# New operation costs and a shared port in the planner that orders a hybrid decoder block's instructions

## The chip, the cores and the metric

The kernel runs on one core of a Trainium2 chip. The metric is the device time of one execution in microseconds (us); lower is better. Times of the kernel before are the median of three runs. The profile shows one further execution, taken by the hardware profiler; its spans and waits are in microseconds from the first instruction.

## The reference, cut to what matters

One layer over 1024 tokens of width 1024, all in float32. The input is normalised and multiplied by one wide matrix. Its columns feed a state-space (SSD) branch of 32 heads in 8 chunks of 128 tokens, a sliding-window attention branch of 12 heads, and two gates. A SwiGLU feed-forward part follows.

```python
h = rmsnorm(x, norm_mix)
z, xBC, dt_raw, qkv, gate_logits = split(h @ w_in)
y_ssm = mamba2_branch(z, xBC, dt_raw, ...) @ w_ssm_out
y_att = dilated_attention_branch(rope(q), rope(k), v) @ w_att_out
gates = sigmoid(gate_logits + b_gate)
x = x + (gates[0] * y_ssm + gates[1] * y_att) @ w_mix_out
h = rmsnorm(x, norm_ffn)
x = x + (silu(h @ w_ffn_gate) * (h @ w_ffn_up)) @ w_ffn_down
return rmsnorm(x, norm_final)
```

## The kernel before, in words

**Arithmetic.** A float32 operand is split into a rounded high part and a low remainder, and a product is made of three TensorE (PE) matmuls over these (`mm3`). The split is a ScalarE (ACT) copy for the high part and a VectorE (DVE) subtraction for the low part. Three groups of products (`Seven` for half of the input columns and for the feed-forward columns, and the last product) use a Strassen-like scheme with seven products in place of eight. They need sums of operands, made by GpSimd (POOL) and DVE.

**Stages.** In the head, eight token tiles `xts[0..7]` of 128 x 1024 are loaded. For each pair of tiles, `stat_task` squares both on ACT with a running sum, multiplies a tile by the norm weights on POOL, and computes the inverse root on DVE in 14 steps on 128 x 2 numbers (`rsqrt_steps`; tiles rv, rt, rs). `tile_task` then scales each tile, transposes it on PE and splits it into `hhi` and `hlo`. `stat_task` of pairs 2 and 3 waits for the events h0 and h2, that is, for tiles 0 and 2 to be emitted. `first_quarter` runs the first two column tiles of the wide product pair by pair, each after its pair's tiles. When half of the tokens is there, `t_first` makes four sums on POOL (`whole`, 128 x 1024 each), and `t_rest` makes eight smaller ones for each quarter of the rest. Then come the columns in the seven-product form (about 130 to 545 us), direct column tiles with the SSD chunks and the attention heads as background (to about 1210), the merge and the mixing product (to about 1600), and the feed-forward part and its last product.

**The order.** The program is written by a planner, `Pace`. Every operation that the code emits passes through `Engine` to `Pace.note`. It asks `cost` for a duration and keeps for each engine the time at which it would be free, for each tile the time at which it would be written (`wr`) and read (`rd`), and for PE a clock `t`. Background work is a set of Python generators (`spawn`). When one yields a list of tiles, `due_at` looks up when these would be written, and the generator goes on when the clock `t` has come to that time: at `due` after every few matmuls of the foreground (`tick`), or at `idle` when the foreground waits for an event (`until`). Of those that are due, the lower `prio` number goes first. So the costs decide only in which order instructions stand in the five engines' queues. On the chip each queue runs in order and waits for its data; the planner's own times appear nowhere in the program. Which work there is, the tiling, the buffers and the order of the foreground's matmuls don't hang on the costs, except that the planner takes buffers as they are freed.

`pump` also uses the clock: it splits the next weights `SLACK` = 4.5 us after they would have landed.

Of the kernel before, what the change touches and what calls it, by code (L numbers as in the profile page):

```python
# [12 lines left out]
F32R = mybir.dt.float32r  # L13
# [4 lines left out]
PSUM = bass.MemoryType.PSUM  # L18
# [64 lines left out]
class Buf:  # L83


    def __init__(self, owner, slot, shape, dt):
        n = math.prod(shape[1:])
        v = slot.tile(dt)[:shape[0], :n]
        if len(shape) == 3:
            v = v.rearrange("p (a b) -> p a b", a=shape[1])  # L90
        elif len(shape) == 4:
            v = v.rearrange("p (a b c) -> p a b c", a=shape[1], b=shape[2])
        self.owner, self.slot, self.v = owner, slot, v
# [43 lines left out]
def _key(a):  # L137
    name = a.tensor.name if hasattr(a, "tensor") else getattr(a, "name", None)
    if name is None:
        return None  # L140
    for big, part in PARTS.items():
        if name.startswith(big) and hasattr(a, "offset"):
            return f"{big}.{part(a.offset)}"
    return name.split("__")[0]


def _free(a):
    return math.prod(a.shape[1:])


def _space(a):
    return a.space if hasattr(a, "space") else a.ap().space
# [29 lines left out]
class Pace:  # L182


    def __init__(self):
        self.t = 0.0
        self.seq = 0
        self.tasks = []
        self.parked = {}
        self.events = set()  # L190
        self.eng = dict.fromkeys(("dve", "act", "pool", "dma"), 0.0)
        self.eng["dma"] = 0.4
        self.wr, self.rd = {}, {}
        self.stall = 0.0

    def cost(self, kind, op, aps, args, kw):
        out = aps[0]
        n = _free(out)
        if kind == "pe":
            if op == "transpose":  # L200
                return 0.11
            return (max(n / 2400, 0.107) if aps[1].dtype == F32R else max(n / 600, 0.107)) + 0.0025
        if kind == "act":
            ptr = sum(1 for k in ("scale", "bias", "accum_out") if hasattr(kw.get(k), "shape"))
            return n / 1200 + 0.095 + 0.08 * ptr
        if kind == "dve":
            if op == "reciprocal":
                return n / 120 + 0.07
            if op == "tensor_reduce":
                n = _free(aps[1])  # L210
            fast = op in ("tensor_copy", "tensor_scalar") and all(_space(a) != PSUM for a in aps[:2])
            return n / (1920 if fast else 960) + 0.07
        if kind == "pool":
            return n * 0.0022 + 0.05
        return n * out.shape[0] * 4 / 360e3

    def note(self, kind, op, aps, args, kw):
        c = self.cost(kind, op, aps, args, kw)
        outs = [_key(aps[0])] + ([_key(kw["accum_out"])] if "accum_out" in kw else [])
        ins = [_key(a) for a in aps[1:]]  # L220
        s = 0.0
        for k in ins + outs:
            t, by = self.wr.get(k, (0.0, kind))
            if by != kind or (kind == "dma" and k in ins):
                s = max(s, t)
            elif kind != "pe":
                s = max(s, t - 0.025)
        for k in outs:
            t, by = self.rd.get(k, (0.0, kind))
            if by != kind:  # L230
                s = max(s, t)
        if kind == "pe":
            self.stall += max(0.0, s - self.t)
            e = self.t = max(self.t, s) + c
            lag = 0.1
        else:
            e = self.eng[kind] = max(self.eng[kind], s) + c
            lag = 2.0 if kind == "dma" else 0.15
        for k in outs:
            self.wr[k] = (e + lag, kind)  # L240
        for k in ins:
            if e >= self.rd.get(k, (0.0, ""))[0]:
                self.rd[k] = (e, kind)

    def due_at(self, bufs):
        return max(self.wr.get(_key(getattr(b, "v", b)), (0.0, ""))[0] for b in bufs)
# [1802 lines left out]
```

## Time and profile before

| what | us |
|---|---|
| median of three runs (lowest and highest) | 2247.75 (2247.21 to 2248.05) |
| the profiled execution | 2249.83 |
| its span, first to last instruction | 2248.0 |
| PE busy in it | 2162.8 |
| DVE, ACT, POOL busy | 1535.9, 877.8, 688.1 |
| mean granted TensorE clock, as a share of full speed | 0.987 |

The profile page names one source line, 165, for every operation, because a helper records them all; tiles are told apart by their names, with the buffer's number left out. A wait in brackets after an instruction is the idle time of its engine before it, with what ended it. A PE that is busy is not always at full speed: the table by stretch has a column with the granted clock.

### The profile page before, as it was taken

To read this page: it belongs to the slowest core of one execution; us is meant where nothing else is said; L and a number is where in the kernel's file an instruction comes from. 1 tells how busy PE (TensorE), PEld (TensorE's weight loads), DVE (VectorE), ACT (ScalarE), POOL (GpSimd) and SP (SyncE) were. 2 spreads that over 40 slices of the span, in tenths; PEclk is the share of its full clock that TensorE was granted. 3 is DMA by queue.
4 is the path that set the end of the run, shared out by engine and by line. 5 is a ranking of instruction groups with operands and counts; after the bars stand their busy time and mean duration, and the time that the engine had idled before them with its cause. 6 is when DMAs were issued, how large, how long until landed. Compare 5 with 4: busy or idle time off the path is not lost.

```text
span 2248.0 us, 27884 instructions
## 1 busy us (share of the span) xinstructions
PE 2162.8 (96%) x10476; PEld 1780.2 (79%) x10476; DVE 1535.9 (68%) x2094; ACT 877.8 (39%) x1565; POOL 688.1 (31%) x420
## 2 busy tenths in 40 slices
PE   4999999999999999999999999999989999999997
PEld 4877888887777778888888887888868877788885
DVE  7879898866777667654343437544796776767788
ACT  3344444434565556433332224322333222224444
POOL 5223343321554445421004003002373344420102
PEclk7999999999999999999999999999999999999998
DMA  3433334336566556431127457454233332349332
GB/s 124 125 89 117 108 116 119 104 112 206 159 191 172 160 169 187 113 94 39 38 72 233 145 178 248 127 173 135 63 108 94 104 107 80 122 155 348 106 95 98
DMA packets 302587, 299.83 MB, mean 133 GB/s; under 512 B 20028, under 2 KB 246260, under 8 KB 302196
## 3 DMA queue, kind: packets, MB, share of 16 engines
q1 hardware_dynamic: 302452, 298.05, 42.7%
q8 instruction: 82, 1.34, 0.3%
q14 instruction: 53, 0.43, 0.1%
HBM read 225.00 MB, written 73.01 MB: 133 GB/s over the span
## 4 chain that ended last, share of the span: by engine, by line
PE 72%; DVE 13%; DMA 5%; issue 4%; ACT 3%; POOL 3%; SPq 0%; DVEq 0%; POOLq 0%; ACTq 0%
DVE rt L165 1%; PE wide__40_16210 L165 1%; PE wide__39_16209 L165 1%; PE wide__39_15720 L165 1%; PE wide__38_15719 L165 1%; PE wide__32_11149 L165 1%; PE wide__33_11380 L165 1%; PE wide__31_11045 L165 1%; PE wide__4_4172 L165 1%; PE wide__29_10493 L165 1%; PE wide__32_11279 L165 1%; PE wide__41_16660 L165 1%; PE wide__35_11736 L165 1%; PE wide__34_11554 L165 1%; PE wide__28_10224 L165 1%
## 5 line engine op out<-in xcount | busy, mean ns | idle before, releaser
L165 POOL TENSOR_TENSOR xr<-xr,nfin 128x512 f32<-128x512 f32 x16 | 22.9, 1443 | 192.2 <-ACT jk L165 192.2
L165 POOL TENSOR_TENSOR slab__24_12098<-h2hi,h2lo 128x1024 f32<-128x1024 f32 x1 | 3.4, 3387 | 135.6 <-PE wide__35_11736 L165 135.6
L165 POOL TENSOR_TENSOR slab__14_10598<-slab__14_10598,last__2_10581 128x1024 f32<-128x1024 f32 x1 | 2.4, 2397 | 122.4 <-DMA slab__14_10598<-yt_d 122.4
L165 POOL TENSOR_TENSOR slab__15_4124<-slab__15_4124,slab__15_4121 128x1024 f32<-128x1024 f32 x1 | 2.3, 2349 | 63.9 <-DVE wide__3_4015 L165 63.9
L165 POOL TENSOR_TENSOR more__3_12094<-h2hi,h2lo 128x512 f32<-128x512 f32 x2 | 2.6, 1294 | 62.3 <-DVE h2lo L165 62.3
L165 POOL TENSOR_TENSOR slab__3_1140<-slab__3_1086 128x512 f32<-128x512 f32 x1 | 1.3, 1297 | 47.5 <-DVE slab__4_1089 L165 47.5
L165 ACT ACTIVATE jk<-xr 128x512 f32<-128x512 f32 x16 | 10.1, 631 | 13.1 <-DVE xr L165 12.8
L165 POOL TENSOR_TENSOR slab__7_7601<-slab__7_7601,slab__33_9400 128x1024 f32<-128x1024 f32 x1 | 2.4, 2393 | 41.0 <-DMA slab__33_9400<-fd 41.0
L165 DVE TENSOR_TENSOR rs<-rs,rt 128x2 f32<-128x2 f32 (+2 forms) x30 | 12.3, 410 | 1.0
L165 PE MATMUL wide__4_4172<-hhi,slab__15_3980 128*128 128x512 f32 x16 | 8.4, 526 | 4.6 <-DVE slab__3_4170 L165 4.6
L165 PE MATMUL bank__3_458<-ident,slab__1_154 128*128 128x128 f32 x4 | 1.1, 428 | 11.5 <-DVE slab__1_154 L165 11.5
L165 POOL TENSOR_TENSOR more__4_12528<-slab__19_12483 128x512 f32<-128x512 f32 x1 | 7.4, 7417 | 14.0 <-DVE slab__25_12501 L165 14.0
L165 ACT ACTIVATE xr<-xr,or 128x512 f32<-128x512 f32 x8 | 5.8, 721 | 14.8 <-DVE or L165 14.0
L165 POOL TENSOR_TENSOR slab__18_8210<-slab__18_8210,slab__15_4121 128x1024 f32<-128x1024 f32 x1 | 2.4, 2397 | 26.6 <-ACT slab__18_8210 L165 26.6
L165 POOL TENSOR_TENSOR slab__11_8494<-slab__11_8494,slab__15_4121 128x1024 f32<-128x1024 f32 x1 | 2.4, 2399 | 26.6 <-ACT slab__11_8494 L165 26.6
L165 POOL TENSOR_TENSOR slab__18_9053<-slab__18_9053,slab__15_4121 128x1024 f32<-128x1024 f32 x1 | 2.4, 2411 | 25.6 <-ACT slab__18_9053 L165 25.6
L165 POOL TENSOR_TENSOR slab__22_8765<-slab__22_8765,slab__15_4121 128x1024 f32<-128x1024 f32 x1 | 2.4, 2406 | 25.5 <-ACT slab__22_8765 L165 25.5
L165 PE MATMUL wide__1_183<-hhi,slab__1_250 128*128 128x256 f32 x32 | 9.8, 307 | 0.3 <-ACT hhi L165 0.3
L165 PE MATMUL wide__1_183<-hlo,slab__1_250 128*128 128x256 f32 x32 | 9.4, 294 | 0.7 <-DVE hlo L165 0.7
L165 PEld LDWEIGHTS bank__3_458<-ident,slab__1_154 128*128 128x128 f32 x4 | 0.7, 218 | 11.7 <-issue 11.7
L165 PE MATMUL wide__1_184<-hhi,slab__1_301 128*128 128x256 f32 x32 | 9.3, 290 | 0.5 <-DVE slab__1_301 L165 0.5
L165 PE MATMUL wide__1_184<-hhi,slab__1_300 128*128 128x256 f32 x32 | 9.5, 297 | 0.0
(7605 smaller groups left out, 8349.3 us busy)
## 6 DMA issues: line engine op xcount, KB each, us to landing
xr<-x_d SPq DMA_DIRECT2D x8, 512.0 KB, 5.8
out<-xr SPq DMA_DIRECT2D x16, 256.0 KB, 2.2
b_d<-hhi SPq DMA_DIRECT2D x1, 1024.0 KB
b_d<-hlo SPq DMA_DIRECT2D x1, 1024.0 KB
slab__1_150<-in_x SPq DMA_DIRECT2D x1, 512.0 KB, 4.2
slab__1_151<-in_x SPq DMA_DIRECT2D x1, 512.0 KB, 5.1
slab__1_158<-in_norm_mix SPq DMA_DIRECT2D x1, 512.0 KB, 5.9
slab__1_165<-in_w_in SPq DMA_DIRECT2D x1, 512.0 KB
```

The costliest lines, as they stand in the source:

```text
L165: r = call(*args, **kw)
```

## The change

Only `Pace` is changed; no operation, tile, wait or event is added or taken away in the code that uses it. `cost` gets other constants: a matmul of split operands on 512 columns goes from 0.216 to 0.226 us, every ACT, DVE and POOL operation gets a fixed part that is larger by about 0.08 to 0.14 us, a float32 matmul with 64 weight columns or fewer becomes cheaper, and DMA goes from 360 to 345 GB/s. A new method, `take_port`, keeps the last 40 intervals of DVE operations whose operands all lie in SBUF and of POOL operations. A new POOL operation that would overlap one of DVE's is moved behind it; a new DVE operation that would overlap one of POOL's is moved by 0.55 of the overlap that is left.

```diff
+        self.port = {k: deque(maxlen=40) for k in ("dve", "pool")}
...
+            if aps[1].dtype == F32R:
+                return max(n / 2400 + 0.0125, 0.107)
+            return max(n / 600, 0.107) * (1.0 if aps[1].shape[-1] > 64 else 0.68) + 0.0025
...
-            return n / 1200 + 0.095 + 0.08 * ptr
+            return n / 1200 + 0.18 + 0.08 * ptr + 0.1 * ("accum_out" in kw)
...
-            fast = op in ("tensor_copy", "tensor_scalar") and all(_space(a) != PSUM for a in aps[:2])
-            return n / (1920 if fast else 960) + 0.07
+            if op in ("tensor_copy", "tensor_scalar") and all(_space(a) != PSUM for a in aps[:2]):
+                return n / 1920 + 0.21
+            return n / 960 + 0.15 + 0.06 * min(ptr, 1)
         if kind == "pool":
-            return n * 0.0022 + 0.05
-        return n * out.shape[0] * 4 / 360e3
+            return n * 0.0022 + 0.15
+        return n * out.shape[0] * 4 / 345e3
...
-            e = self.eng[kind] = max(self.eng[kind], s) + c
+            s = max(self.eng[kind], s)
+            if kind == "pool" or kind == "dve" and all(_space(a) != PSUM for a in aps):
+                s = self.take_port(s, c, kind)
+            e = self.eng[kind] = s + c
...
+    def take_port(self, s, c, kind):
+        other = self.port["dve" if kind == "pool" else "pool"]
+        for a, e in other:
+            if a < s + c and s < e:
+                s += (e - s) * (0.55 if kind == "dve" else 1.0)
+        self.port[kind].append((s, s + c))
+        return s
```

## Rows read from the trace of the kernel before

**Rows 1.** Page: PE's busy time, and its share in 40 equal slices, tenths.
```profile
PE 2162.8 (96%) x10476; PEld 1780.2 (79%) x10476; DVE 1535.9 (68%) x2094; ACT 877.8 (39%) x1565; POOL 688.1 (31%) x420
...
PE   4999999999999999999999999999989999999997
```

**Rows 2.** Table by stretch: length, busy us (instructions) of each engine, PE clock, DMA, GB/s.
```profile
0.00:72.00 72.00, 42.15 (x279) 40.18 (x280) 51.13 (x90) 23.72 (x38) 37.67 (x22) 0.81 0.32 103
...
120.00:200.00 80.00, 70.56 (x292) 56.16 (x291) 67.46 (x74) 32.22 (x49) 27.68 (x16) 0.96 0.32 94
...
580.00:930.00 350.00, 339.39 (x2125) 273.76 (x2124) 249.47 (x408) 196.54 (x446) 171.42 (x124) 1.00 0.57 170
...
1380.00:1420.00 40.00, 36.06 (x157) 28.90 (x156) 27.39 (x28) 16.05 (x30) 7.04 (x3) 1.00 0.56 182
...
1600.00:1660.00 60.00, 53.21 (x274) 43.99 (x273) 57.95 (x59) 24.29 (x39) 35.97 (x18) 1.00 0.28 84
1660.00:2000.00 340.00, 336.73 (x1476) 276.12 (x1475) 246.38 (x320) 99.04 (x176) 151.35 (x104) 1.00 0.32 104
...
2210.00:2248.00 38.00, 21.43 (x77) 15.44 (x75) 29.53 (x104) 14.02 (x29) 9.31 (x8) 0.79 0.29 110
sum 2248.00, PE 2162.76 PEld 1780.21 DVE 1535.91 ACT 877.78 POOL 688.09; mean PE 166.37 PEld 136.94 DVE 118.15 ACT 67.52 POOL 52.93
```

**Rows 3.** Chain that ended last: start us, us, what (12 matmuls).
```profile
195.16 2.72 PE bank__13_1512 L165 x12
```

**Rows 4.** Timeline near 130 us: start us, us, instruction [idle before, releaser].
```profile
131.52 0.69 DVE L165 TENSOR_TENSOR slab__3_1071<-slab__2_694,slab__3_1071 128x512 fp32r<-128x512 f32 x1
...
132.58 0.62 ACT L165 CAST slab__4_1089<-slab__2_793 128x512 fp32r<-128x512 f32 x1
...
135.16 1.30 POOL L165 TENSOR_TENSOR slab__3_1140<-slab__3_1086 128x512 f32<-128x512 f32 x1 [47.52 <-DVE slab__4_1089 L165]
```

**Rows 5.** Timeline of the head, first and second pair of tiles.
```profile
15.11 1.15 ACT L165 ACTIVATE slab__1_151<-slab__1_151,rs 128x1024 f32<-128x1024 f32 x1 [4.11 <-DVE rs L165]
...
16.17 1.04 ACT L165 ACTIVATE slab__1_160<-slab__1_152 128x1024 f32<-128x1024 f32 x1
...
17.38 2.36 POOL L165 TENSOR_TENSOR slab__1_152<-slab__1_152,slab__1_158 128x1024 f32<-128x1024 f32 x1 [3.96 <-ACT slab__1_160 L165]
...
19.64 0.45 PE L165 MATMUL wide__1_183<-hhi,slab__1_250 128*128 128x256 f32 x1
...
20.89 2.39 POOL L165 TENSOR_TENSOR slab__1_153<-slab__1_153,slab__1_158 128x1024 f32<-128x1024 f32 x1 [1.15 <-DMA slab__1_143<-in_consts]
...
22.26 2.10 DVE L165 TENSOR_TENSOR slab__1_301<-slab__1_169,slab__1_300 128x1024 fp32r<-128x1024 f32 x1 [0.25 <-ACT slab__1_300 L165]
...
24.28 2.35 DVE L165 TENSOR_SCALAR rv<-sq 128x2 f32<-128x2 f32 x1
```

**Rows 6.** Timeline of the head, third and fourth pair of tiles.
```profile
37.06 2.37 POOL L165 TENSOR_TENSOR slab__1_156<-slab__1_156,slab__1_158 128x1024 f32<-128x1024 f32 x1 [8.15 <-ACT slab__1_160 L165]
...
39.49 2.31 DVE L165 TENSOR_TENSOR rs<-rs,rt 128x2 f32<-128x2 f32 x1
...
48.64 2.33 POOL L165 TENSOR_TENSOR slab__1_675<-hhi,hlo 128x1024 f32<-128x1024 f32 x1
...
48.74 2.25 DVE L165 TENSOR_TENSOR rs<-rs,rt 128x2 f32<-128x2 f32 x1
...
53.12 1.09 PE L165 MATMUL bank__3_458<-ident,slab__1_154 128*128 128x128 f32 x4 [11.54 <-DVE slab__1_154 L165]
...
56.48 1.28 POOL L165 TENSOR_TENSOR slab__1_678<-hhi,hlo 128x512 f32<-128x512 f32 x1 [5.51 <-DVE hlo L165]
...
63.92 0.63 PE L165 MATMUL bank__4_547<-ident,slab__1_156 128*128 128x128 f32 x4 [1.08 <-DVE slab__1_156 L165]
```

**Rows 7.** Waits of PE, 580 to 930: total us, times, longest.
```profile
PE bank__86_6731 L165 <- DVE slab__26_6624 L165: 1.8, 1, 1.8
...
PE bank__83_6556 L165 <- DVE half__13_6421 L165: 0.3, 1, 0.3
```

More of the change, by code (lines that the diff above doesn't have):

```diff
@@ L198, in cost @@
         n = _free(out)
+        ptr = sum(1 for v in list(args) + list(kw.values()) if hasattr(v, "shape") and _free(v) == 1 and n > 1)
         if kind == "pe":
@@ L201, in cost @@
                 return 0.11
-            return (max(n / 2400, 0.107) if aps[1].dtype == F32R else max(n / 600, 0.107)) + 0.0025
+            if aps[1].dtype == F32R:
+                return max(n / 2400 + 0.0125, 0.107)
+            return max(n / 600, 0.107) * (1.0 if aps[1].shape[-1] > 64 else 0.68) + 0.0025
         if kind == "act":
-            ptr = sum(1 for k in ("scale", "bias", "accum_out") if hasattr(kw.get(k), "shape"))
-            return n / 1200 + 0.095 + 0.08 * ptr
+            return n / 1200 + 0.18 + 0.08 * ptr + 0.1 * ("accum_out" in kw)
         if kind == "dve":
             if op == "reciprocal":
-                return n / 120 + 0.07
+                return n / 120 + 0.15
             if op == "tensor_reduce":
                 n = _free(aps[1])
-            fast = op in ("tensor_copy", "tensor_scalar") and all(_space(a) != PSUM for a in aps[:2])
-            return n / (1920 if fast else 960) + 0.07
+            if op in ("tensor_copy", "tensor_scalar") and all(_space(a) != PSUM for a in aps[:2]):
+                return n / 1920 + 0.21
+            return n / 960 + 0.15 + 0.06 * min(ptr, 1)
         if kind == "pool":
-            return n * 0.0022 + 0.05
-        return n * out.shape[0] * 4 / 360e3
+            return n * 0.0022 + 0.15
+        return n * out.shape[0] * 4 / 345e3
     def note(self, kind, op, aps, args, kw):
```

## The prediction

> **What bounds the kernel now.** Read the page's busy time and slices first [rows 1]: PE is busy for 2162.8 of 2248.0 us, and only the first and the last slice stand well below nine tenths. A change that adds and removes no work can win only PE's idle 85.2 us (2248.0 - 2162.8) and the time in which PE has the lower clock. So the second view is the table by stretch, with length minus PE busy [rows 2]: 29.9 us idle in the head (0 to 72, at a mean clock of 0.81), 9.4 in the start of the seven-product stage (120 to 200), 10.6 under the SSD chunks (580 to 930), 3.9 at the change to the mixing product (1380 to 1420), 6.8 in the start of the feed-forward part (1600 to 1660), 3.3 in its steady part (1660 to 2000), 16.6 in the tail (2210 to 2248). Together 80.5; the other 4.7 is in the stretches not shown. The third view is what ended each wait. The last is the durations of single operations, against the costs in the diff.
>
> **The new costs against the trace.** Twelve matmuls on 512 columns take 2.72 us, 0.2267 each [rows 3]; the old cost is 512/2400 + 0.0025 = 0.2158, the new 0.2258. On 512 elements the trace has 0.69 us for DVE, 0.62 for ACT, 1.30 for POOL [rows 4]; old 0.60, 0.52, 1.18, new 0.68, 0.61, 1.28. So the new planner sees what single operations take within 2%, where the old was 5 to 16% short. That is no gain by itself: the planner's times don't reach the chip, only the order does. An instruction that PE has in its queue before its data is ready stalls everything behind it; one that comes later costs nothing while other matmuls stand in between. So stalls by too early emission can go, and stalls of a foreground that has nothing else to do can't, unless DVE, ACT or POOL get another order.
>
> **Part 1, the head.** PE has no other work here, so what counts is the order on the other three engines.
> With the old costs a step of the inverse root is 0.07 us plus 0.15 of delay, less 0.025 within DVE; 14 steps end at 9.65 on the planner's clock, just before tile 2's data is due (0.4 + 0.18 + 5 loads of 1.46 + 2.0 = 9.86). So ACT scales tile 1 first and squares tile 2 after it. The trace shows it: scaling at 15.11, square at 16.17, POOL's product of tile 2 at 17.38 and of tile 3 at 20.89, the low part of the second weights at 22.26, and only then the second pair's chain, at 24.28 [rows 5].
> With the new costs a step is about 0.15 + 0.15, so 14 steps from 7.0 need at least 4.2 us and end after 11.2, and with the port they are pushed behind POOL's two operations to well after 13. Tile 2 is due at 0.4 + 0.19 + 5 x 1.52 + 2.0 = 10.2, tile 3 at 11.7, the second weights at 13.2. So squares 2 and 3, POOL's products 2 and 3 and the split of the second weights now stand ahead of the end of the first chain.
> On the chip that has a price and a gain. The price: a tiny DVE step that falls in a POOL operation takes 2.25 to 2.35 us [rows 5, 6], so two products (2.36 and 2.39) and the split (2.10) can put the first chain back by up to 6.9 us, and the first matmul from 19.64 to about 26. The gain: the second pair's chain, started at 24.28 now, starts near 16 (tile 3 due near 12, a square of 1.04, one or two POOL operations of 2.36), about 8 us earlier, and runs interleaved with the first.
> The end of the head is set by the last pair. Now the third chain runs against six POOL operations in a row, from 37.06 to 51 (two products, four sums of `t_first`): five steps from 39.49 to 48.74 take 2.3 us each, and PE waits 11.5 us for tile 4 [rows 6]. In the new order pairs 2 and 3 still wait for h0 and h2, so POOL's eight operations (four products, four sums, 8 x 2.35 = 18.8 us) still meet these chains; with tile 0 emitted near 27 they end near 46.5, and the fourth chain after them near 51, against about 63 now (its tile is transposed at 63.92). 63 - 51 = 12 is the best of it. The four sums at 56.48, 1.28 us each, can block the last steps as they do now: minus 5.1. What is left is 6.9; I take 5, because both figures rest on POOL having no pause. Bounds: the first matmul 6.9 later and nothing given back, +7; and 12 earlier, -12.
>
> The Trainium skill (SBUF — State Buffer, "SBUF: two separate sides") says that the port pair that DVE and GpSimd share is an exclusive lock, held for a whole instruction, and that the loser blocks fully. The five steps of 2.3 us agree. The change moves a DVE step by only 0.55 of what is left of POOL's operation, so by that rule it still sees several steps fit into one; the rival "ramps" below is what that would mean.
>
> **Part 2, under the SSD chunks.** The wait table of this stretch has 13 waits of PE, from 1.8 down to 0.3 us, almost all for a DVE, ACT or POOL result of a chunk or of rotary [rows 7]. Units of independent matmuls stand around them, and the PE as a whole is at 339 of 350. A chunk's chain between two PE steps has three to eight operations that the old costs make 0.08 to 0.1 us too short each, 0.3 to 0.8 in sum, before any blocking: the size of the waits. Later emission removes these. It also lengthens each chunk in the planner, but the y of the SSD is not used before the merge, hundreds of us later. I take -4 of 10.6; bounds -10 (all) and +3 (waits move to other places, about a third of today's).
>
> **Part 3, the other stretches.** In 120 to 200 and 1600 to 1660 DVE is busy for 67.5 of 80 and 58.0 of 60 us [rows 2]: it is the bound, the seven products come in a fixed order, and the work is the same. I take 0, bounds -3 and +5 for the first, -3 and +4 for the second. The steady feed-forward part idles 3.3 us in 340: -1, since its operations are as short in the old costs as the others, bounds -3 and +3. The mixing change (3.9) and the rest (4.7) I take at 0, bounds together -6 and +5. In the tail all waits are for a chain that is serial on DVE after the last matmul: 0, bounds -1 and +2. No DMA, wait or buffer is added; SP's order follows the same events, and its queue is far from full in every row of the table.
>
> **Sum.** -5 - 4 - 1 = -10 on the profiled execution's 2249.83 gives 2239.8. That execution lies 2.1 us above the median of the runs (2247.75), so for the median 2237.8, say 2238. All bounds at once are -38 and +29; they are independent stretches, so I take about half.
>
> **The rivals.**
> - *Ramps*: the order moves, but the head still ends with one DVE step for each POOL operation and the ramps stay DVE's. For it: six POOL operations back to back with the third chain [rows 6]. Against: the 13 waits under the SSD have no such limit. Part 2 alone with other small losses, -3: about 2245.
> - *Slower head*: POOL's products 2 and 3 and the second split go into the first chain, the first matmul comes at 26 in place of 19.64, and the third and fourth chains meet POOL as before, so the 6.9 us are not given back. For it: POOL idles now from 13.4 to 17.38, when the last steps of the first chain run freely. Against: the second chain's 8 us. It decides when the last pair's transposes come later than 63.92. Price +7, part 2 half gone at -2, and +1 elsewhere: 2254.
> - *All waits of early emission go*: the head gives its full 12, the SSD stretch 8, the others 3: -23, 2225. For it: the new costs are within 2%. Against: DVE at 58 of 60.
> - That the change doesn't reach the program at all is excluded: already the squares of tiles 2 and 3 change places by the arithmetic above.
>
> **How the numbers follow.** This kernel's measurement can tell 0.2%, 4.5 us, from no change: faster is below 2243.3, slower above 2252.2. Forecast 0.48 (its own range 2229 to 2247), ramps 0.16, slower head 0.26, all waits 0.10. Faster: 0.43 of the forecast, 0.10, 0.04 of the ramps, 0.01 of the slower head = 0.58. Same: 0.05 + 0.11 + 0.03 = 0.19. Slower: 0.22 + 0.01 = 0.23. A range of 2219 to 2257 leaves out 1 in 10 on either side.
>
> **What would show it.** Right: ACT's squares of tiles 2 and 3 ahead of the scaling of tile 1; the first matmul later than 19.64, the last pair's transposes before 60; under 7 us idle from the SSD's first chunk to its last; DVE still near full in both ramps. Wrong: transposes of the last pair after 64, or new PE waits of over 1 us between the chunks.

## The result, and the profile after

The changed kernel takes 2229.63 us (median of four runs, 2226.1 to 2232.08) against 2247.9 (four runs of the kernel before on the same chip): 0.9918 of it, 95% interval 0.9901 to 0.9935, or 18.3 us less. The forecast was 10 less; the sign, the likeliest case and the range held, but most of the gain is not where the forecast put it. The profiled execution is the lowest of the four, at 2226.1, so its sum reads -23.7 against the profiled execution before. The terms of single stretches below come from one profiled execution of each kernel, and the four timed runs lie 6 us apart, so terms are good to a few us at best.

The page after, as [rows 1]: the same number of counted instructions on every engine; PE is busy 8.4 us less, and the span is 23.7 us shorter.

```profile
PE 2154.4 (97%) x10476; PEld 1781.7 (80%) x10476; DVE 1545.7 (69%) x2094; ACT 879.5 (40%) x1565; POOL 690.9 (31%) x420
...
PE   5999999999999999999999999999999999999996
```

The table by stretch after, over the stretches of [rows 2] (length, busy us and instructions of PE, PEld, DVE, ACT, POOL, PE clock, DMA share, GB/s):

```profile
0.00:72.00 72.00, 41.61 (x277) 39.24 (x278) 51.84 (x90) 23.75 (x38) 36.82 (x22) 0.83 0.30 98
120.00:200.00 80.00, 73.23 (x304) 58.41 (x303) 67.42 (x76) 33.57 (x52) 31.57 (x16) 0.96 0.35 103
...
580.00:930.00 350.00, 350.00 (x2120) 287.76 (x2117) 245.09 (x376) 191.59 (x422) 164.69 (x110) 1.00 0.53 161
...
1600.00:1660.00 60.00, 53.51 (x222) 43.22 (x221) 58.52 (x63) 23.93 (x37) 26.97 (x16) 0.94 0.25 76
1660.00:2000.00 340.00, 340.00 (x1502) 281.71 (x1501) 246.76 (x319) 103.44 (x177) 147.99 (x102) 1.00 0.34 111
```

The head idles as long as before (30.4 against 29.9). Under the SSD PE does not idle at all (10.6 before), nor in the steady feed-forward part (3.3). The trap of this table: a fixed window of time holds other work in a kernel that is faster. So the stretches are cut at fixed work from here on. The 81 accumulators called `wide` come in the same order in both kernels; the first matmul of the 8th (the first direct column tile) and of the 45th (the last SSD and attention work is then done) bound the same matmuls. The table by stretch between these two, kernel before and kernel after:

```profile
553.40:1184.11 630.71, 620.10 (x3541) 507.83 (x3542) 380.61 (x573) 304.20 (x661) 228.42 (x151) 1.00 0.44 129
```
```profile
552.09:1168.20 616.11, 616.03 (x3541) 508.40 (x3542) 386.30 (x573) 302.77 (x661) 234.88 (x150) 1.00 0.44 131
```

Both have 3541 matmuls. Idle time goes from 10.61 to 0.08 us, busy time falls by 4.07: 14.6 together. The granted clock is the same. DVE and POOL are even busier than before, but PE no longer waits for them.

Where the 4.07 us lie can be read from the trace. Three matmuls of the kernel before, the last one ahead of a wait:

```profile
826.95 0.39 PE L165 MATMUL wide__10_6672<-hlo,slab__19_6322 128*128 128x512 f32 x1
827.18 0.39 PE L165 MATMUL wide__10_6672<-hhi,slab__19_6323 128*128 128x512 f32 x1
829.41 1.09 PE L165 MATMUL bank__86_6731<-slab__26_6624,half__13_6642 128*64 128x128 f32 x16 [1.84 <-DVE slab__26_6624 L165]
```

Matmuls follow each other every 0.23 us although each is shown with 0.39. Ahead of a wait the 0.39 count in full: from 827.18 to the next start it is 2.23 us, of which only 1.84 are shown as idle. Added up, the matmuls directly ahead of and behind the stretch's 23 waits take 6.5 us more, from start to start, than the median of their shape. In the changed kernel one wait is left and 0.6 us of this kind; all other matmuls take 1.8 more there. So the fall in busy time lies at the waits that have gone.

How it does so is seen in the middle of the stretch. The timeline at the first matmul of the 25th `wide` accumulator, before and after:

```profile
917.32 0.39 PE L165 MATMUL wide__13_7592<-hhi,slab__22_7279 128*128 128x512 f32 x1
```
```profile
870.10 0.40 PE L165 MATMUL wide__13_7094<-hhi,slab__21_6828 128*128 128x512 f32 x1
```

The last number of a name counts the tiles handed out so far. The same column tile now comes 47 us earlier and 498 tiles earlier: the chunks have been put back behind the foreground. Over the kernels of the next section that change the costs, this tile number and PE's idle time between the two bounds fall together: 7592 and 10.6 us before, 7588 and 9.1 in e2, 7409 and 7.3 in e3, 7341 and 1.3 in e4, 7169 and 1.7 in e8, 7094 and 0.1 in the changed kernel. Two don't fit by the number alone: e1 (7152) has 8.2, of which 6.7 are one wait of another kind, and e10 (7089) still has 3.0. At the 45th accumulator both kernels stand at tile 9454 again, the changed one 15.9 us ahead.

The next table gives each kernel's difference to the kernel before, between the first matmuls of the 5th, 8th, 45th, 75th and 76th `wide` accumulator (118.1, 553.4, 1184.1, 1611.5 and 2047.6 us before) and the end of the span, all from profiled executions; the last two columns are the timed medians' difference and the ratio's interval. Labels are those of the next section.

| kernel | head | seven products | SSD | mixing | feed-forward (start and steady part) | rest | timed | 95% interval |
|---|---|---|---|---|---|---|---|---|
| after | -0.2 | -1.1 | -14.6 | -0.6 | -4.1 | -3.0 | -18.3 | 0.9901 to 0.9935 |
| e1_costs | +0.6 | -2.7 | -4.2 | +2.0 | -5.2 | -1.5 | -8.4 | 0.995 to 0.9974 |
| e2_port | +1.1 | -5.8 | -4.1 | +4.1 | -4.7 | -1.8 | -8.9 | 0.9947 to 0.9976 |
| e3_pe | +0.8 | +6.1 | -4.2 | +3.1 | +0.7 | +1.4 | +11.0 | 1.0036 to 1.0069 |
| e4_fixed | -1.4 | -0.3 | -12.6 | +2.8 | -7.0 | -3.5 | -19.8 | 0.9901 to 0.9944 |
| e5_ssd_only | -0.4 | -1.0 | -15.2 | +1.8 | -0.6 | -0.1 | -14.3 | 0.9911 to 0.995 |
| e6_late_sums | -7.3 | +1.6 | -14.5 | -0.9 | -4.1 | -2.8 | -26.4 | 0.9861 to 0.9897 |
| e7_no_pool_head | -11.5 | -2.3 | -16.0 | -1.3 | -3.0 | -3.1 | -30.8 | 0.9843 to 0.9874 |
| e8_fixed_port | -0.2 | -2.3 | -14.1 | -2.3 | -5.8 | -2.0 | -24.0 | 0.9876 to 0.9905 |
| e9_fixed_port_head | -14.2 | -1.6 | -14.0 | -0.9 | -5.5 | -2.0 | -32.8 | 0.9833 to 0.9863 |
| e10_full_lock | +2.2 | +9.7 | -12.5 | +0.5 | -1.8 | -1.5 | -5.1 | 0.9964 to 0.9983 |
| e11_old_head | -0.4 | -1.2 | -15.3 | +2.1 | -2.5 | -3.0 | -21.6 | 0.9888 to 0.9917 |

The head after, against [rows 5, 6], in the timeline. First two pairs:

```profile
11.39 1.06 ACT L165 ACTIVATE slab__1_160<-slab__1_152 128x1024 f32<-128x1024 f32 x1 [0.29 <-DMA slab__1_152<-in_x]
...
15.76 1.21 DVE L165 TENSOR_TENSOR slab__1_257<-slab__1_169,slab__1_256 128x1024 fp32r<-128x1024 f32 x1
15.78 3.39 POOL L165 TENSOR_TENSOR slab__1_153<-slab__1_153,slab__1_158 128x1024 f32<-128x1024 f32 x1
...
20.86 1.15 ACT L165 ACTIVATE slab__1_151<-slab__1_151,rs 128x1024 f32<-128x1024 f32 x1 [5.40 <-DVE rt L165]
...
25.15 0.36 PE L165 MATMUL wide__1_183<-hhi,slab__1_242 128*128 128x256 f32 x1
```

The square of tile 2 stands at 11.39, ahead of the scaling of tile 1 (20.86), POOL's product of tile 3 and the second split lie inside the first chain, and the first matmul of the product comes at 25.15 instead of 19.64. Third and fourth pair:

```profile
36.12 2.37 POOL L165 TENSOR_TENSOR slab__1_156<-slab__1_156,slab__1_158 128x1024 f32<-128x1024 f32 x1 [4.22 <-ACT slab__1_160 L165]
...
40.80 2.39 POOL L165 TENSOR_TENSOR slab__1_670<-hhi,hlo 128x1024 f32<-128x1024 f32 x1
40.90 2.32 DVE L165 TENSOR_SCALAR rt<-rt 128x2 f32<-128x2 f32 x1
...
43.16 2.33 POOL L165 TENSOR_TENSOR slab__1_671<-hhi,hlo 128x1024 f32<-128x1024 f32 x1
43.25 2.25 DVE L165 TENSOR_TENSOR rs<-rs,rt 128x2 f32<-128x2 f32 x1
...
52.30 1.09 PE L165 MATMUL bank__3_479<-ident,slab__1_154 128*128 128x128 f32 x4 [9.50 <-DVE slab__1_154 L165]
...
63.15 1.09 PE L165 MATMUL bank__4_547<-ident,slab__1_156 128*128 128x128 f32 x4 [2.92 <-DVE slab__1_156 L165]
```

POOL's six operations still run back to back from 36.12, one 128 x 2 step of DVE for each, and the last pair is transposed at 63.15, against 63.92.

### The profile page after: what moved, and what is told of

It reads as the page before. It is cut to its first block, busy times and chain, and to the rows that moved or that the text cites. A ratio compares the mean times of both kernels' runs of the same rounds, so it can differ in the third digit from the quotient of the medians.

```text
span 2224.3 us, 27832 instructions
## 1 busy us (share of the span) xinstructions
PE 2154.4 (97%) x10476; PEld 1781.7 (80%) x10476; DVE 1545.7 (69%) x2094; ACT 879.5 (40%) x1565; POOL 690.9 (31%) x420
## 5 line engine op out<-in xcount | busy, mean ns | idle before, releaser
L165 POOL TENSOR_TENSOR slab__11_10598<-slab__11_10598,last__2_10581 128x1024 f32<-128x1024 f32 x1 | 2.5, 2501 | 122.1 <-DMA slab__11_10598<-yt_d 122.1
L165 POOL TENSOR_TENSOR slab__15_4124<-slab__15_4124,slab__14_4121 128x1024 f32<-128x1024 f32 x1 | 2.3, 2339 | 63.2 <-DVE wide__3_4015 L165 63.2
L165 POOL TENSOR_TENSOR slab__21_7103<-slab__21_7103,slab__32_9422 128x1024 f32<-128x1024 f32 x1 | 2.4, 2388 | 43.1 <-DMA slab__32_9422<-fd 43.1
L165 POOL TENSOR_TENSOR slab__3_1145<-slab__3_1086 128x512 f32<-128x512 f32 x1 | 1.6, 1554 | 43.3 <-PE bank__6_1094 L165 43.3
L165 PEld LDWEIGHTS bank__1_281<-ident,slab__1_151 128*128 128x128 f32 x4 | 0.7, 217 | 12.9 <-ACT slab__1_151 L165 12.9
L165 POOL TENSOR_TENSOR slab__22_9025<-slab__22_9025,slab__14_4121 128x1024 f32<-128x1024 f32 x1 | 2.4, 2404 | 25.8 <-ACT slab__22_9025 L165 25.8
L165 DVE TENSOR_TENSOR rt<-rt,rv 128x2 f32<-128x2 f32 (+2 forms) x30 | 9.7, 324 | 0.7
L165 PE MATMUL wide__1_183<-hhi,slab__1_242 128*128 128x256 f32 x32 | 9.5, 295 | 0.7 <-ACT hhi L165 0.7
L165 ACT ACTIVATE xr<-xr,or 128x512 f32<-128x512 f32 x8 | 5.8, 719 | 10.6 <-DVE or L165 10.5
L165 DVE TENSOR_SCALAR rv<-sq 128x2 f32<-128x2 f32 x4 | 2.4, 608 | 10.6 <-ACT slab__1_161 L165 10.6
L165 POOL TENSOR_TENSOR slab__10_8743<-slab__10_8743,slab__14_4121 128x1024 f32<-128x1024 f32 x1 | 2.4, 2406 | 22.7 <-ACT slab__10_8743 L165 22.7
```

The lines of the kernel that those rows point to most:

```text
L165: r = call(*args, **kw)
```

## The experiments

Diffs are against the changed kernel unless another is named. Every kernel was timed against runs of the kernel before on its own chip, and the chips differ; so two kernels are compared by their differences to the kernel before.

**Which costs carry the gain.** The five kernels of this part split the change.

`e1_costs`: all new costs, no port.

```diff
-            if kind == "pool" or kind == "dve" and all(_space(a) != PSUM for a in aps):
-                s = self.take_port(s, c, kind)
```

> All new constants, take_port taken out. Theory (the SSD stretch gains because honest fixed parts of ACT, DVE and POOL put PE's instructions behind their data): most of the gain stays, -12 to -18 us against the kernel before, and PE idle between 580 and 930 is under 3 us. Rival (the shared port is what matters): less than half stays, -8 to 0.

Measured 0.9962, 8.4 us less: between the two ranges. The SSD stretch gives only 4.2, because of one wait; the waits of PE, 580 to 960 (us in total, times, longest), and the timeline at the wait:

```profile
PE wide__15_7817 L165 <- DVE slab__6_7815 L165: 6.7, 1, 6.7
PE wide__8_5338 L165 <- DVE slab__4_5293 L165: 1.3, 1, 1.3
```
```profile
936.32 3.15 POOL L165 TENSOR_TENSOR slab__20_7773<-slab__20_7773,slab__15_4121 128x1024 f32<-128x1024 f32 x1 [2.64 <-ACT slab__20_7773 L165]
...
947.46 1.23 DVE L165 TENSOR_TENSOR wide__14_7589<-wide__14_7589,slab__16_4119 128x1024 f32<-128x1024 f32 x1 [0.33 <-ACT slab__20_7811 L165]
948.60 1.22 DVE L165 TENSOR_TENSOR slab__6_7815<-wide__14_7449,slab__20_7773 128x1024 f32<-128x1024 f32 x1
...
949.97 0.77 PE L165 MATMUL wide__15_7817<-hhi,slab__23_7542 128*128 128x512 f32 x1 [6.73 <-DVE slab__6_7815 L165]
```

There are two `wide` accumulators. A column tile's first matmul waits until DVE has read one of them (`wide__14_7449`) out in a rotary step. That step's other operand was there at 939.47 (936.32 + 3.15), but in DVE's queue it stands behind a step on the next accumulator, which itself had to wait for ACT. Of the chunks' waits, one of 1.3 and one of 0.2 are left (1.4 us idle from 580 to 930, as the theory has it). So the costs alone remove nearly all waits of the chunks. Why the rotary step stands so late is not shown: e4 below has no port either, and no such wait.

`e2_port`: `take_port` alone; every constant of `cost` as before.

```diff
-            return n / 960 + 0.15 + 0.06 * min(ptr, 1)
+            return n / (1920 if fast else 960) + 0.07
...
-            return n * 0.0022 + 0.15
+            return n * 0.0022 + 0.05
```

> take_port alone, old constants. Theory: 0 to -6 us, PE idle between 580 and 930 stays above 6. Rival (the port is what matters): -10 to -18, PE idle there under 4.

Measured 0.9962, 8.9 us less, again between the two ranges. Under the SSD nearly all waits stay, as the theory says, with PE busy for 340.89 of 350 in the table by stretch:

```profile
580.00:930.00 350.00, 340.89 (x2122) 276.82 (x2121) 255.70 (x412) 197.48 (x444) 173.21 (x121) 1.00 0.55 168
1660.00:2000.00 340.00, 340.00 (x1502) 281.56 (x1501) 249.42 (x321) 103.64 (x176) 151.36 (x104) 1.00 0.34 113
```

The port helps in the stretches where POOL and DVE both make sums (seven products -5.8, feed-forward -4.7). Under the SSD it takes only 1.5 of the 10.6 us of waits away, though the stretch is 4.1 shorter, and the mixing loses 4.1.

`e3_pe`: the two new matmul costs alone.

```diff
-            return n * 0.0022 + 0.15
-        return n * out.shape[0] * 4 / 345e3
+            return n * 0.0022 + 0.05
+        return n * out.shape[0] * 4 / 360e3
...
-                s = self.take_port(s, c, kind)
```

> The two PE costs alone (0.226 in place of 0.216 for a matmul on 512 columns, 0.68 of a float32 matmul on 64 weight columns). Theory: a dearer matmul makes the planner think that more time passes for each, so background instructions come earlier, not later: 0 to +6 us, PE idle between 580 and 930 at 10 or more. Rival (planner and chip must agree on PE's pace first): -5 to -12.

Measured 1.0052: slower by 11. The sign is the theory's, the reason is not. By the theory the chunks come earlier. The trace shows them later: at the first matmul of the 25th column tile 183 fewer tiles have been handed out than before the change.

```profile
903.82 0.48 PE L165 MATMUL wide__13_7409<-hhi,slab__20_7150 128*128 128x512 f32 x1
```

The SSD stretch has not more waits but fewer (4.7 us idle from 580 to 930, the stretch -4.2). The loss lies in the seven products (+6.1) and the mixing (+3.1). The cost of the 512-column matmul is nearer to the trace than before, and yet the order is worse; no run parts the two costs.

`e4_fixed`: the fixed parts of DVE, ACT and POOL alone; matmul and DMA costs as before, no port.

```diff
-            if aps[1].dtype == F32R:
-                return max(n / 2400 + 0.0125, 0.107)
+            return (max(n / 2400, 0.107) if aps[1].dtype == F32R else max(n / 600, 0.107)) + 0.0025
...
-                s = self.take_port(s, c, kind)
```

> The new costs of ACT, DVE and POOL alone; PE, DMA old, no port. Theory: -12 to -20 us, the SSD stretch as good as with the whole change or better. Rival (PE's pace or the port needed too): -6 to 0.

Measured 0.9922, 19.8 us less, as much as the whole change. The table by stretch has the SSD with 1.3 us of waits and the steady part with none; the 25th column tile comes 31 us and 251 tiles earlier than before the change:

```profile
580.00:930.00 350.00, 348.73 (x2151) 283.84 (x2151) 253.20 (x398) 196.02 (x439) 170.75 (x121) 1.00 0.56 172
1660.00:2000.00 340.00, 340.00 (x1501) 281.62 (x1500) 250.57 (x322) 103.63 (x176) 147.13 (x101) 1.00 0.35 112
```
```profile
886.71 0.80 PE L165 MATMUL wide__13_7341<-hhi,slab__22_7005 128*128 128x512 f32 x1
```

`e8_fixed_port`: these fixed parts and the port, matmul and DMA costs as before.

```diff
-                return max(n / 2400 + 0.0125, 0.107)
+            return (max(n / 2400, 0.107) if aps[1].dtype == F32R else max(n / 600, 0.107)) + 0.0025
...
-        return n * out.shape[0] * 4 / 345e3
+        return n * out.shape[0] * 4 / 360e3
```

> The new costs of ACT, DVE and POOL, with the port; PE and DMA at the old costs. Theory (the fixed parts carry the gain, the port adds little on top): -16 to -23, within 4 of the fixed parts alone. Rival (the port's -9 adds to the fixed parts' -20): -26 to -30.

Measured 0.989, 24.0 us less, between the two ranges: 5.7 us better than the whole change by the medians (2.9 by the profiled spans), which fits that the matmul and DMA costs take something back; the intervals (0.9876 to 0.9905 and 0.9901 to 0.9935) overlap, so its size is not settled.

**Where the gain is.** `e5_ssd_only`: the new costs and the port only from the start of the SSD's preparation (the first line) to the merge (the second).

```diff
+    pace.new = True
...
+    pace.new = False
```

> The new costs and the port only while the SSD and attention work is emitted (from the return of the saved half of the input to the merge); the old ones before and after. Theory (the SSD stretch gives most, and its gain stands by itself): -11 to -16 us, head and start of the seven products as before the change. Rival (the gain is made by the order that comes in from the earlier stages): -5 to 0.

Measured 0.9931, -14.3, with -15.2 in the SSD stretch and all others near their old values. The gain of this stretch stands by itself; it is not the head's order that brings it.

`e11_old_head`: the reverse for the head, old costs and no port until the seven products begin (the second line).

```diff
+        self.new = False
...
+    pace.new = True
```

> The old costs and no port until the two column tiles of the head are through and the seven-product stage begins, the changed ones after that. Theory that the head gained nothing (first matmul 5.7 later, third pair's transposes at the same time, end of the head 0.3 later): within 3 us of the changed kernel, with the first wait at 15.9 as before and the last pair's transposes at 63.9. The prediction's head term, in which the order of the head is worth 5: 4 to 6 us slower than the changed kernel.

Measured 0.9902, with 16.16 for the first transposes and 63.76 for the last pair's. Without the new head the change is not slower, by the medians 3.3 faster, with overlapping intervals. The head's new order is worth nothing.

**Why the head gave nothing.** `e6_late_sums`: POOL's four sums of the first half are emitted after those of the second half.

```diff
+            if self.tag == "in":
+                return
+            self.t_sums()
...
+            if self.tag == "in":
+                self.t_sums()
```

> The whole change, and the four POOL sums of the first half of the tokens emitted after those of the second half. Theory (the head gained nothing because these four sums, in POOL's queue behind the products, hold the third pair's chain at one DVE step per sum): the third chain ends near 43 in place of 51, the last pair is transposed near 55 in place of 63, and the total is 6 to 10 below the change, -24 to -28 against the kernel before. Rival (the chain is late by DVE's own queue): the third chain stays after 49, total within 3 of the change.

Measured 0.9879, 26.4 us less and 8.1 better than the changed kernel by the medians. In the profiled execution the head is 7.1 shorter and the seven products 2.7 longer. The same chain in the timeline:

```profile
38.99 2.40 POOL L165 TENSOR_TENSOR slab__1_157<-slab__1_157,slab__1_158 128x1024 f32<-128x1024 f32 x1
```
```profile
39.08 2.32 DVE L165 TENSOR_TENSOR rt<-rt,rv 128x2 f32<-128x2 f32 x1
...
41.44 0.17 DVE L165 TENSOR_SCALAR rt<-rt 128x2 f32<-128x2 f32 x1
...
43.22 0.16 DVE L165 TENSOR_TENSOR rs<-rs,rt 128x2 f32<-128x2 f32 x1
```
```profile
44.38 0.63 PE L165 MATMUL bank__3_479<-ident,slab__1_154 128*128 128x128 f32 x4 [1.06 <-DVE slab__1_154 L165]
```

The step that meets POOL's last product takes 2.32, and from 41.4, with POOL idle, the rest of the chain is through in 2 us at 0.16 a step. PE's 9.50 us of waiting for tile 4 become 1.06, and the last pair is transposed at 54.32.

`e7_no_pool_head`: e6, and the norm weights of tiles 2 to 7 multiplied on DVE, in the operation that scales the tile. The diff is against e6.

```diff
-            if q or i:
+            if 2 * q + i == 1:
...
-        if i == 0:
+        if i != 1:
+            yield [nm]
             nc.vector.scalar_tensor_tensor(xt.v, xt.v, rs, nm.v, ALU.mult, ALU.mult)
...
-            nc.vector.tensor_scalar(xt.v, xt.v, rs, None, ALU.mult)
```

> As the run with the late sums, and the multiplication of tiles 2 to 7 by the norm weights goes from POOL into DVE's scaling (scalar_tensor_tensor, as tile 0 has it): 1.28 in place of 0.75 us for a tile on DVE, six POOL operations of 2.4 us less. Theory (POOL's lock sets the whole head): the chains run at 0.2 us a step, the last pair is transposed before 50, the head ends near 55 in place of 72: 15 to 20 below the change, -33 to -38 against the kernel before. Rival (DMA or DVE's queue comes next): no more than 3 better than the late sums alone.

Measured 0.9858, 30.8 us less: 4.4 better than e6, but less than expected. The last pair is transposed at 48.30, as the theory has it. The timeline of POOL and the waits of PE in the head say why:

```profile
41.23 1.29 POOL L165 TENSOR_TENSOR slab__1_668<-hhi,hlo 128x512 f32<-128x512 f32 x1 [27.75 <-DVE hlo L165]
```
```profile
PE bank__1_277 L165 <- ACT slab__1_151 L165: 10.0, 1, 10.0
PE bank__4_541 L165 <- DVE slab__1_156 L165: 3.4, 1, 3.4
PE bank__6_715 L165 <- DVE slab__1_660 L165: 3.1, 1, 3.1
```

The last pair's chain still meets POOL's sums of 1.29 from 41.23 (3.4 us of waiting), and the sums that were put back now hold the weight split of a product that comes next (3.1).

`e9_fixed_port_head`: the costs of e8 with the head of e7.

```diff
-                return max(n / 2400 + 0.0125, 0.107)
+            return (max(n / 2400, 0.107) if aps[1].dtype == F32R else max(n / 600, 0.107)) + 0.0025
...
+            if 2 * q + i == 1:
```

> The fixed parts of DVE, ACT and POOL and the port, with the old costs of matmuls and DMAs (e8: -24.0 against before), and with the head of e7 (four sums of the first half late, norm weights of tiles 2 to 7 multiplied on DVE). Theory that head and SSD stretch are separate: e7's head was worth -13.3 beside the change, so about -24 - 13 = -37, near 2210. Rival, that a head which ends earlier moves the background's order in all later stages, so that gains don't add (e7 already fell 4 short of its sum): -28 to -31, 2216 to 2219, no better than e7. Read from the first wait (10.0 in e7), the last pair's transposes (48.3 in e7) and PE's idle time from 580 to 930 (none in the changed kernel).

Measured 0.9848, 2215.22 us. It is faster than the kernel before and the changed one, but by the timed runs it can't be told from e7 (0.9843 to 0.9874): the head is worth 8.8 on top of e8, not 13. At -32.8 it lies between the theory's -37 and the rival's -28 to -31. In the profiled execution head and SSD do add (-14.2 in the head, the SSD unchanged at -14.0), which speaks against the rival's reason.

**How much of the lock to charge.** `e10_full_lock`: a DVE operation waits in the planner for all that is left of POOL's.

```diff
-                s += (e - s) * (0.55 if kind == "dve" else 1.0)
+                s += (e - s) * 1.0
```

> The change with 0.55 replaced by 1.0: in the planner a DVE operation waits for the whole of POOL's rest. If the lock as the chip shows it (a 128 x 2 step of 2.3 us for each POOL operation) is what the order should know, the better model gives less waiting: -2 to -6 against the changed kernel, 2224 to 2228. Rival, that the size of the charge hardly matters once the fixed parts are right (e4, without any port, is within 2.2 us of the whole change): within 4.5 us of the changed kernel's 2229.6, with either sign.

Measured 0.9974: 13 us worse than the changed kernel, and both theories are wrong. The loss is 10.8 in the seven products, where the waits of PE from 150 to 270 are for the partial sums `own` on DVE, each of which reads an accumulator of PE out; the changed kernel has 3.9 and 0.4 for them there:

```profile
PE bank__9_1349 L165 <- DVE own__3_1242 L165: 4.8, 1, 4.8
...
PE bank__9_1370 L165 <- DVE own__2_1241 L165: 1.9, 1, 1.9
```

What the trace shows is that these sums come late in DVE's queue, not how the larger charge puts them there. Where between 0.55 and 1.0 it turns was not tried.

## Why the prediction was right, and where it was not

**Direction and total.** Forecast -10, measured -18.3. The likeliest case, with a sum of three gains, had the right sign, and its own range (2229 to 2247) held by 0.6 us. In part this is luck: the head was taken 5 too good and the SSD stretch some 10 too bad, and the two misses go against each other. The rival *ramps* is half true (the third chain keeps one step for each POOL operation), *all waits* is true under the SSD and false in the head, and *slower head* is not true: the first matmul did come 5.5 later, but this was given back. Of the signs named, the squares' place, the late first matmul, under 7 us idle under the SSD (0 from 580 to 930) and DVE near full in both ramps (67.42 of 80, 58.52 of 60) came as told; the last pair before 60 did not.

**Part 1, the head: the step that failed.** The order moved as worked out, and so did the first matmul ("about 26", 25.15). The second pair's chain also started earlier, at 13.90 in place of 24.28. But this was not kept: the pair's first transposes, before and after, stand at the same place.

```profile
32.53 1.08 PE L165 MATMUL bank__2_371<-ident,slab__1_152 128*128 128x128 f32 x4 [5.21 <-DVE slab__1_152 L165]
```
```profile
32.60 0.63 PE L165 MATMUL bank__2_377<-ident,slab__1_152 128*128 128x128 f32 x4 [0.71 <-DVE slab__1_152 L165]
```

The last steps of that chain stand in DVE's queue behind the low parts of the first pair, and so fall into the third pair's products, which run from 27.14 and 29.50: a step takes 2.36 there, and the scaling of tile 2 takes 2.78 in place of 0.76. The next thing that failed is "with tile 0 emitted near 27 they end near 46.5", which rests on POOL having no pause. Tile 2 fires h2; the squares of tile 6 stand in ACT's queue behind the casts of tile 2, and POOL's product of tile 6 starts only at 36.12, after an idle 4.22:

```profile
27.14 2.40 POOL L165 TENSOR_TENSOR slab__1_154<-slab__1_154,slab__1_158 128x1024 f32<-128x1024 f32 x1 [7.97 <-ACT slab__1_160 L165]
29.50 2.40 POOL L165 TENSOR_TENSOR slab__1_155<-slab__1_155,slab__1_158 128x1024 f32<-128x1024 f32 x1
```
```profile
27.21 2.36 DVE L165 TENSOR_TENSOR rs<-rs,rt 128x2 f32<-128x2 f32 x1
...
29.67 2.78 DVE L165 TENSOR_SCALAR slab__1_152<-slab__1_152,rs 128x1024 f32<-128x1024 f32 x1
```

So six POOL operations end at 50.08 (47.75 + 2.33) and not 46.5, and the third chain is where it was. The fourth does not end with them either: four of its steps meet the smaller sums, from 56.52 to 61.52, and its tile is scaled at 62.25. Term -5, measured -0.2; e6, e7 and e11 show it from three sides. The rule of the Trainium skill (SBUF — State Buffer, "SBUF: two separate sides") that the loser of the shared port blocks fully agrees with the steps of 2.32 that become 0.16 in e6. It was still no recipe for the planner: charged in full, in e10, it cost 13 us.

**Part 2, the SSD stretch: the term that was mis-sized.** "Later emission removes these" is what happened (47 us and 498 tiles at the 25th accumulator), and e4 and e5 show that the DVE, ACT and POOL costs do nearly all of it (12.6 of 14.6) and that the stretch does it alone. I took -4 of 10.6, with -10 as the bound for all waits. All went, 10.5, and a further 4.1 of busy time. So the visible idle time was no bound: a wait takes more than the idle time that is shown for it, as the matmuls beside the waits show. That the amount by which a chain was too short (0.3 to 0.8) would remove only part of each wait was a guess: the trace shows no wait left at all.

**Part 3.** Seven products: 0, measured -1.1. This hides that the parts go against each other there: port -5.8, matmul costs +6.1. Feed-forward: 0 for its start and -1 for its steady part, measured -4.1 together. Cut once more, at the first matmul of the same accumulator (1663.64 and 1648.61), before and after:

```profile
1611.47:1663.64 52.17, 45.38 (x194) 35.53 (x193) 50.76 (x55) 21.70 (x34) 30.99 (x16) 1.00 0.29 89
1663.64:2047.58 383.94, 380.67 (x1669) 312.29 (x1668) 270.08 (x351) 112.94 (x200) 155.18 (x107) 1.00 0.38 125
```
```profile
1594.93:1648.61 53.68, 47.19 (x195) 37.97 (x193) 53.54 (x53) 21.57 (x33) 27.40 (x16) 0.94 0.21 64
1648.61:2026.93 378.32, 378.32 (x1670) 313.18 (x1668) 272.66 (x353) 117.70 (x201) 156.15 (x107) 1.00 0.38 126
```

The start is 1.5 longer, with a granted clock of 0.94 in place of 1.00, and the steady part is 5.6 shorter, above its 3.3 of visible idle time as under the SSD. e4 and e2 each do the latter alone, and e5, where the old costs hold, has -0.6 in the whole of the feed-forward part. Mixing 0, measured -0.6. The tail 0, measured -3.0: four waits of PE for the last operands (3.6 in all) fell to two of 0.2. They stood ahead of the last matmul, and the prediction was wrong to put all of the tail behind it. The granted clock is 0.53 of full speed from 2221 to 2228 before, behind these waits, and 1.00 in the changed kernel from 2196.9 to the last matmul; that one ends 6.6 us earlier by fixed work, and 3.6 are lost again, because what follows it takes 16.5 in place of 12.9; why it does is not shown.

**What stays open.** Why the new matmul costs by themselves make the order worse is not settled; e3 says only where, and that the chunks did not come earlier. Nor is it settled why charging the whole lock makes it worse. Of the 5.4 between the profiled -23.7 and the timed -18.3, 3.5 are that the profiled execution after lies below its median, and 1.9 that the one before lies above its own.

## What to carry to other kernels

Where a planner only sets an order, ask of each constant whether it makes background work come earlier or later, and read the answer from the trace. Here some 0.1 us more on each DVE, ACT and POOL operation, which put the chunks 251 tiles later by the 25th column tile, was worth as much as the whole change, while matmul costs meant to be nearer to the chip lost 11 us and a fuller model of the lock 13. Price a stretch by cutting both traces at the same work, since windows of equal time hide what has moved, and don't take visible idle time as the most that it can give. And when small serial DVE steps set the time, look for GpSimd work that can go elsewhere before improving their order: moving four sums gave 8 us, re-ordering around them none.

## What the runs showed of the hardware that was not expected

- A 128 x 2 step on DVE takes 0.16 us with POOL idle. While POOL works through 1024 columns, one step for each of its operations takes 2.25 to 2.36. It goes the other way too: POOL's product at 15.78 takes 3.39 instead of 2.36 beside a DVE split of 1.21.
- The same 3541 matmuls were busy for 620.1 us with 10.6 us of waits among them and for 616.0 without: a wait that is shown with 1.84 us put 2.23 between two starts that else lie 0.23 apart.
- In e1's wait PE idles from 943.24 to 949.97. The granted clock is 1.00 of full speed (2.4 GHz) from 940 to 945, 0.53 from 945 to 950, and behind the wait, with PE busy throughout, still 0.50 (1.2 GHz) from 950 to 955; from 955 to 960 it is 0.94:

```profile
950.00:955.00 5.00, 5.00 (x13) 3.50 (x13) 1.15 (x1) 1.25 (x2) 3.42 (x2) 0.50 0.09 34
```
